# Work on fetched expert rows tied to units of the dense product, and the next norm's rows loaded later

## The chip, the cores and the metric

The kernel runs on one core of a Trainium2 chip. A core has five engines that run side by side: TensorE (PE in the profile; PEld is its weight load), VectorE (DVE), ScalarE (ACT), GpSimd (POOL) and SyncE (SP). Transfers are issued from a queue of SyncE (SPq) or GpSimd (POOLq) and run on 16 shared DMA engines. The metric is the device time of one execution in microseconds; lower is better.

## The reference

Two blocks run one after the other on 256 tokens of width 1024, in float32. The first (two layers of feed-forward, convolution and differential attention) is untouched here. The second has two layers; each is a mixer followed by an expert layer, and the change is in the expert layer:

```
q      = (ht @ w_query).reshape(T, 8, 2, 128)
scores = einsum('thpd,hpkd->thpk', q, sub_keys)          # 128 keys a half
s_top, i_top = top_k(scores, 16)
best, pos    = top_k(s_top[0] + s_top[1], 16)            # all pairs of the two halves
expert_idx   = i_top[0] * 128 + i_top[1]                 # at pos
gates        = softmax(best)
a   = gelu(einsum('tkd,td->tk', expert_u[expert_idx], x)) * gates
out = einsum('tk,tkd->td', a, expert_v[expert_idx])
```

A token so uses 8 x 16 = 128 of 16384 experts; an expert is a row of 1024 numbers in `expert_u` and one in `expert_v`. Between layers stand norms with a gain (and, in the second block, a scale and a shift that depend on a condition vector).

## The kernel before

**Two ways through the experts.** In each expert layer the last 160 tokens (`ND`) go the dense way: all 16384 experts are applied to them. The weights come as 128 units of 128 experts for each of the two products. A unit of the first product is 8 matmuls (16 instructions in the trace, line 1402), a gelu on ScalarE, and later a multiplication with the gates; a unit of the second product is 8 matmuls into three PSUM accumulators (line 1419). The first 96 tokens (`NS`) go the sparse way: `fetch` (line 1321) issues an indirect DMA on GpSimd's queue which brings 128 chosen rows, one to a partition, into one of ten buffers (`NGATHER`), and `fetched` (line 1336) works on a row tile: 96 steps on u (line 1344: multiply with the token's activation and sum) and then 96 steps on v (line 1349: multiply with the gate and add). Step i, once issued, is followed by the fetch for step i + 10, which reuses its buffer.

**What sets the pace.** `sparse(n)` is called after unit n (0 to 127 first product, 128 on second product) and issues steps until their number is 192 (n + 1 - begun - LAG_S) / (250 - begun - LAG_S). A fetch carries a dependence on the last matmul issued before it (`paced[-1]`), so it waits on the chip for that unit. A step carries none: it waits for its row tile alone.

**What sets the order on an engine.** The code issues instructions in program order, but outside the attention stage a scheduler orders each engine's queue by when it estimates an instruction to be ready, earlier program position first. On the chip each queue is worked in that fixed order, and an instruction that waits holds all behind it. `behind` (line 1188) adds an order to such a pair without a wait.

**What runs beside the first product.** VectorE finds the top 16s of the remaining heads and tokens (`halves`, `pick`, `Choice`); these pieces lie in a list with prices (`later`), from which each unit takes 1.3 (`PUMP_U`). The heads of tokens 0 to 127 are chosen in two groups of four. Six units after the last choice the softmax is issued (`LAG_E`, lines 1171 and 1193 to 1195), four units later (`LAG_T`) TensorE transposes indices and gates (lines 1200 to 1202), and then 20 groups of 8 tokens get one-hot tiles on VectorE (lines 1226 to 1229), a gate product on TensorE (1238, 1239), and its application on VectorE and ScalarE (1252, 1254).

**Rows of the next norm.** `gains(ph)` (line 453) loads the gain of the next stage's norm to all partitions (512 KB written) from SyncE's queue and, where the norm has a condition, the scale too; two empty items of 2.0 and then `scaled` (line 466, on VectorE) go to the list; after `scaled` the shift is loaded into the scale's buffer, again from SyncE's queue. Layer 0's expert stage does this for the spatial stage (`sgu`, with scale and shift), layer 1's for the final norm (gain alone). SyncE's queue also issues all weight loads (line 299): 1 MB for two units, into three buffers (`RAW`).

Of the kernel before, what the change touches and what calls it, by code (L numbers as in the profile page):

```python
# [16 lines left out]
ALU = mybir.AluOpType  # L17
# [4 lines left out]
P = 128  # L22
# [25 lines left out]
AFTER = mybir.DependencyInfo(mybir.DependencyClass.Sync, mybir.DependencyReason.SCHED_ONLY)  # L48
# [4 lines left out]
NGATHER = 10  # L53
# [1 line left out]
TOPK = 16  # L55
NCAND = 80
LAG_P, LAG_A = 1, 2
LAG_E, LAG_T, LAG_S = 6, 4, 5
PUMP_Q, PUMP_U = 1.6, 1.3
GSCALE = 2.0 ** 14  # L60
NEG = -3.0e38
# [296 lines left out]
class Kernel:  # L358
# [635 lines left out]
    def peer(s, ph):  # L994
# [9 lines left out]
        V, S, mm = nc.vector, nc.scalar, nc.tensor.matmul  # L1004
        l = int(ph[5:])
        with s.tc.tile_pool(name=ph, bufs=1, reuse_waits="tile") as pp:
            def tl(shape, tag, name=None, dt=F32, bufs=1):
                return pp.tile(list(shape), dt, tag=tag, name=f"{name or tag}_{ph}", bufs=bufs)
# [174 lines left out]
            unit, lagged, gelus = 0, [], []  # L1183
# [98 lines left out]
            ix, z, gate, act = (tl((P, NS), n, dt=d) for n, d in (("ix", U32), ("z", F32), ("eg", F32), ("act", F32)))  # L1282
            steps = [(k, c) for k in 'uv' for c in range(NS)]
            hb, sums, got, paced, known = [], [], [], [], []
            count = 0
# [35 lines left out]
            def fetch(i):  # L1321
                if i < len(steps):
                    kind, c = steps[i]
                    while c // GS not in known:
                        s.pump(1.0)
                    f = nc.gpsimd.indirect_dma_start(out=got[i % NGATHER], out_offset=None, in_=A[f'peer_{kind}'],  # L1326
                                                     in_offset=bass.IndirectOffsetOnAxis(ap=ix[:, c:c + 1], axis=0))
                    if paced:
                        s.tc.add_manual_dep(f.ins, paced[-1].ins.name, AFTER,
                                            reason="a fetch goes with its unit of the dense part")  # L1330

            def acted(c0, c1):
                S.activation(act[:, c0:c1], z[:, c0:c1], AF.Gelu_apprx_tanh)
                V.tensor_tensor(act[:, c0:c1], act[:, c0:c1], gate[:, c0:c1], op=ALU.mult)

            def fetched(n):

                nonlocal count
                while count < min(n, len(steps)):
                    i = count  # L1340
                    (kind, c), row = steps[i], got[i % NGATHER]
                    part = int(c % GS >= 32)
                    if kind == 'u':
                        V.tensor_tensor_reduce(out=row, in0=row, in1=hb[part], scale=1.0, scalar=0.0, op0=ALU.mult,  # L1344
                                               op1=ALU.add, accum_out=z[:, c:c + 1])
                    elif c in (0, 32):
                        V.tensor_scalar(sums[part], row, act[:, c:c + 1], None, op0=ALU.mult)
                    else:
                        V.scalar_tensor_tensor(sums[part], row, act[:, c:c + 1], sums[part], op0=ALU.mult, op1=ALU.add)  # L1349
                    if kind == 'u' and c in (71, 95):  # L1350
                        acted(*((0, GS) if c == 71 else (GS, NS)))
                    fetch(i + NGATHER)
                    count += 1

            first, second = Choice(0, 0, 4, 16), Choice(0, 4, 8, 16)
# [22 lines left out]
            Choice(1, 0, PH, end - 8).queue()  # L1378
            s.later(0.0, chosen.append, 1)
            s.later(0.0, after, LAG_E, softmax)  # L1380
            s.gains(s.following)


            begun, last = [], 2 * P - 6
# [1 line left out]
            def sparse(n):  # L1386

                if known:
                    if not begun:
                        begun.append(n)  # L1390
                        for i in range(NGATHER):
                            fetch(i)
                    fetched(len(steps) * (n + 1 - begun[0] - LAG_S) // (last - begun[0] - LAG_S))
                s.st.ahead()

            for j in range(P):
# [8 lines left out]
                unit = j  # L1405
# [6 lines left out]
            dense = [s.acc(f"acc_{ph}_{i}") for i in range(3)]  # L1412

            def column(c):
                return dense[c // 3][:, (c % 3) * ND:(c % 3 + 1) * ND]

            def add(j, w, ts):
                for c in range(8):
                    paced.append(mm(column(c)[:, ts], w[:, c * P:(c + 1) * P], ring[:, j, ts], start=j == c % 3 == 0,  # L1419
                                    stop=j == P - 1, skip_group_check=True))  # L1420

            for j in range(P - 4):
                add(j, s.st.next(), slice(0, ND))
                sparse(P + j)


            fetched(len(steps))
            s.flush()
            s.next_norm(s.following)
# [6 lines left out]
            out = [s.work(f"out{i}_{ph}") for i in range(2)]  # L1436
# [634 lines left out]
```

## Time and profile before

| | |
|---|---|
| median of 3 runs | 2895.89 us (2894.49 to 2901.7) |
| profiled execution | 2900.55 us, its span 2898.8 us |
| TensorE busy, mean granted clock | 96% of the span, 0.983 |
| VectorE, ScalarE, GpSimd busy | 66%, 33%, 19% |
| first product, layer 0 and layer 1 | starts at 1308.0 and 2239.6 us |
| second product, layer 0 and layer 1 | starts at 1650.7 and ends at 1955 us; layer 1 ends at 2884 us |

The page cuts the span into 40 slices of 72.5 us; the expert layers fill slices 18 to 26 and 31 to 40. A granted clock of 1.00 is 2.4 GHz, 0.50 is 1.2 GHz; a value between is a mean over the stretch. A DMA share near 1 says that the 16 DMA engines were busy all the time. A busy TensorE is not TensorE at its peak, so stretches are compared by how long the same number of matmuls takes.

### The profile page before, as it was taken

How to read it: one execution, taken by the hardware profiler on the slowest of the kernel's cores; microseconds unless marked ns; L12 is line 12 of the kernel's file. 1: busy time of each engine (PE TensorE's matmuls, PEld its weight loads, DVE VectorE, ACT ScalarE, POOL GpSimd, SP SyncE). 2: the span in 40 equal slices, each digit the busy share in tenths (PEclk: the TensorE clock that was granted, in tenths of full speed). 3: DMA queues.
4: the chain of work that ended last, by engine and by line, in shares of the span. 5: the costliest groups of instructions: out<-in, count | busy, mean ns of one | idle time of the engine just before them, and what ended most of it. 6: DMA issues, size and time to landing. Idle time of an engine off the chain costs nothing. (4 is left out here: it accounts for less than half of the span.)

```text
span 2898.8 us, 46472 instructions
## 1 busy us (share of the span) xinstructions
PE 2773.7 (96%) x18628; PEld 2567.5 (89%) x18628; DVE 1903.9 (66%) x3574; ACT 946.2 (33%) x1922; POOL 544.2 (19%) x522
## 2 busy tenths in 40 slices
PE   9999999999999999999789999999999969999998
PEld 7988799899879988889789999997988969999997
DVE  5858785785878676578787544436668878644442
ACT  6457644544654454441121100014444112100000
POOL 0001100000110000004533433310001443334340
PEclk9999999999999999999899999999999989999998
DMA  7844385685438654448989999966444989999994
GB/s 260 329 178 167 139 317 207 224 306 175 168 115 326 214 195 164 170 168 323 370 309 362 415 415 415 413 265 240 175 172 146 382 341 338 368 402 415 415 414 159
DMA packets 146761, 802.44 MB, mean 277 GB/s; under 512 B 18622, under 2 KB 20030, under 8 KB 82281
## 3 DMA queue, kind: packets, MB, share of 16 engines
q1 hardware_dynamic: 87856, 590.67, 54.1%
q0 software_dynamic: 58688, 208.81, 18.7%
q8 instruction: 146, 2.39, 0.3%
q14 instruction: 71, 0.57, 0.1%
HBM read 795.76 MB, written 1.88 MB: 275 GB/s over the span
## 5 line engine op out<-in xcount | busy, mean ns | idle before, releaser
L272 ACT CAST whi<-wraw 128x1024 fp32r<-128x1024 f32 (+1 forms) x508 | 515.2, 1019 | 843.8 <-DMA wraw<-in_w 281.7
L280 DVE TENSOR_TENSOR wlo<-wraw,whi 128x1024 fp32r<-128x1024 f32 (+1 forms) x508 | 597.2, 1181 | 284.1 <-ACT whi L272 282.3
L1402 PE MATMUL pu_peer<-hT_peer,wraw 128*128 128x160 f32 x4096 | 580.6, 303 | 34.0 <-DMA wraw<-in_w 30.0
L1402 PEld LDWEIGHTS pu_peer<-hT_peer,wraw 128*128 128x128 f32 x4096 | 567.5, 193 | 38.6 <-issue 24.9
L1419 PE MATMUL acc_peer<-ring_peer,wraw 128*128 128x160 f32 (+2 forms) x4224 | 583.5, 300 | 13.4 <-DMA wraw<-in_w 11.5
L1419 PEld LDWEIGHTS acc_peer<-ring_peer,wraw 128*128 128x128 f32 x4224 | 576.1, 192 | 21.2 <-DMA wraw<-in_w 15.6
L1349 DVE SCALAR_TENSOR_TENSOR whis_peer<-wlos_peer,act_peer,whis_peer 128x1024 f32<-128x1024 f32 x72 | 92.7, 1287 | 116.5 <-DMA wlos_peer<-in_peer_v,ix_peer 116.4
L628 PE MATMUL pg_ffn<-hhi_first,wlo 128*128 128x256 f32 x576 | 164.4, 285 | 0.0
L627 PE MATMUL pg_ffn<-hlo_first,whi 128*128 128x256 f32 x576 | 163.9, 284 | 0.0
L626 PE MATMUL pg_ffn<-hhi_first,whi 128*128 128x256 f32 x576 | 163.6, 284 | 0.0
L628 PE MATMUL pu_ffn<-hhi_first,wlo 128*128 128x256 f32 x576 | 163.5, 284 | 0.0
L627 PE MATMUL pu_ffn<-hlo_first,whi 128*128 128x256 f32 x576 | 163.2, 283 | 0.0
L626 PE MATMUL pu_ffn<-hhi_first,whi 128*128 128x256 f32 x576 | 162.2, 282 | 0.0
L1344 DVE CUSTOM_DVE_ANT_0 wlos_peer<-wlos_peer,whis_peer 128x1024 f32<-128x1024 f32 x80 | 97.4, 1224 | 61.2 <-DMA wlos_peer<-in_peer_u,ix_peer 60.9
L727 DVE SCALAR_TENSOR_TENSOR ada<-adaw,ca,ada 128x1536 f32<-128x1536 f32 x64 | 116.2, 1816 | 30.4 <-DMA adaw<-in_ada_w 30.3
L1264 ACT ACTIVATE ring_peer<-pu_peer 128x160 f32<-128x160 f32 (+13 forms) x186 | 51.3, 276 | 229.2 <-PE pu_peer L1402 229.2
L1326 POOL DMA_INDIRECT wlos_peer<-in_peer_u,ix_peer x80 | 101.4, 1268 | 110.1 <-PE pu_peer L1402 66.9
L626 PEld LDWEIGHTS pg_ffn<-hhi_first,whi 128*128 128x128 f32 x576 | 109.9, 191 | 4.0 <-issue 1.1
L627 PEld LDWEIGHTS pg_ffn<-hlo_first,whi 128*128 128x128 f32 x576 | 109.5, 190 | 2.8
L628 PEld LDWEIGHTS pg_ffn<-hhi_first,wlo 128*128 128x128 f32 x576 | 109.8, 191 | 0.0
L626 PEld LDWEIGHTS pu_ffn<-hhi_first,whi 128*128 128x128 f32 x576 | 109.2, 190 | 0.0
L628 PEld LDWEIGHTS pu_ffn<-hhi_first,wlo 128*128 128x128 f32 x576 | 108.8, 189 | 0.0
(617 smaller groups left out, 5331.6 us busy)
## 6 DMA issues: line engine op xcount, KB each, us to landing
wraw<-in_w SPq DMA_DIRECT2D x500, 1024.0 KB, 6.7
adaw<-in_ada_w SPq DMA_DIRECT2D x64, 768.0 KB, 7.2
gain_ffn<-in_ffn_norm SPq DMA_DIRECT2D x4, 512.0 KB, 5.6
ring_peer<-in_keysT POOLq DMA_DIRECT2D x2, 1024.0 KB, 5.1
bi_sgu<-in_sgu_b_in POOLq DMA_DIRECT2D x6, 256.0 KB, 7.7
wlos_peer<-in_peer_u,ix_peer POOLq DMA_INDIRECT x80, 10.9
wlos_peer<-in_peer_v,ix_peer POOLq DMA_INDIRECT x72, 12.6
x<-in_x SPq DMA_DIRECT2D x2, 512.0 KB
```

The source lines that it names most:

```text
L272: K.nc.scalar.copy(whi[:, c], s.raw_of(u)[:, c])
L280: K.nc.vector.tensor_tensor(wlo[:, c], s.raw_of(u)[:, c], whi[:, c].bitcast(F32), op=ALU.subtract)
L626: mm(ps, wh, s.hhi[:, k, :], start=k == 0, stop=False)
L627: mm(ps, wh, s.hlo[:, k, :], start=False, stop=False)
L628: mm(ps, wl, s.hhi[:, k, :], start=False, stop=k == 7)
L727: nc.vector.scalar_tensor_tensor(a, raws.pop(i), ca[:, k:k + 1], a, op0=ALU.mult, op1=ALU.add)
L1264: gelus.append(S.activation(slot[:, g:], ps[:, g:], AF.Gelu_apprx_tanh))
L1326: f = nc.gpsimd.indirect_dma_start(out=got[i % NGATHER], out_offset=None, in_=A[f'peer_{kind}'], in_offset=bass.IndirectOffsetOnAxis(ap=ix ...
L1344: V.tensor_tensor_reduce(out=row, in0=row, in1=hb[part], scale=1.0, scalar=0.0, op0=ALU.mult, op1=ALU.add, accum_out=z[:, c:c + 1])
L1349: V.scalar_tensor_tensor(sums[part], row, act[:, c:c + 1], sums[part], op0=ALU.mult, op1=ALU.add)
L1402: paced.append(mm(pu, w[:, k * P:(k + 1) * P], hT[:, k, :], start=k == 0, stop=k == 7))
L1419: paced.append(mm(column(c)[:, ts], w[:, c * P:(c + 1) * P], ring[:, j, ts], start=j == c % 3 == 0, stop=j == P - 1, skip_group_check=True))
```

## The change

- `LAG_S` goes from 5 to 8: the first step comes three units later, and the rate of steps to units rises so that the last step stays where it was.
- Each VectorE step in `fetched` gets the dependence that the fetch has: it waits on the chip for the last matmul issued before it.
- `gains(following)` is no longer called before the first product; it is called at unit 32 (`P // 4`) of the second product, whose loop now takes 1.0 from the list at each unit.

The choice in two groups of heads is the same in both kernels.

```diff
-LAG_E, LAG_T, LAG_S = 6, 4, 5
+LAG_E, LAG_T, LAG_S = 6, 4, 8
...
-                    if paced:
-                        s.tc.add_manual_dep(f.ins, paced[-1].ins.name, AFTER,
-                                            reason="a fetch goes with its unit of the dense part")
+                    pace(f)
+
+            def pace(i):
+
+                if paced:
+                    s.tc.add_manual_dep(i.ins, paced[-1].ins.name, AFTER, reason="paced by the dense part")
...
                     if kind == 'u':
-                        V.tensor_tensor_reduce(out=row, in0=row, in1=hb[part], scale=1.0, scalar=0.0, op0=ALU.mult,
-                                               op1=ALU.add, accum_out=z[:, c:c + 1])
+                        i = V.tensor_tensor_reduce(out=row, in0=row, in1=hb[part], scale=1.0, scalar=0.0, op0=ALU.mult,
+                                                   op1=ALU.add, accum_out=z[:, c:c + 1])
                     elif c in (0, 32):
-                        V.tensor_scalar(sums[part], row, act[:, c:c + 1], None, op0=ALU.mult)
+                        i = V.tensor_scalar(sums[part], row, act[:, c:c + 1], None, op0=ALU.mult)
                     else:
-                        V.scalar_tensor_tensor(sums[part], row, act[:, c:c + 1], sums[part], op0=ALU.mult, op1=ALU.add)
+                        i = V.scalar_tensor_tensor(sums[part], row, act[:, c:c + 1], sums[part], op0=ALU.mult,
+                                                   op1=ALU.add)
+                    pace(i)
...
-                    fetch(i + NGATHER)
+                    fetch(count + NGATHER)
...
             s.later(0.0, after, LAG_E, softmax)
-            s.gains(s.following)
...
             for j in range(P - 4):
                 add(j, s.st.next(), slice(0, ND))
+                if j == P // 4:
+                    s.gains(s.following)
+                s.pump(1.0)
                 sparse(P + j)
```

## Rows read from the trace of the kernel before

**Rows 1.** The page, parts 1 and 2: TensorE's busy time and transfer rate of 40 slices.

```profile
PE 2773.7 (96%) x18628; PEld 2567.5 (89%) x18628; DVE 1903.9 (66%) x3574; ACT 946.2 (33%) x1922; POOL 544.2 (19%) x522
...
GB/s 260 329 178 167 139 317 207 224 306 175 168 115 326 214 195 164 170 168 323 370 309 362 415 415 415 413 265 240 175 172 146 382 341 338 368 402 415 415 414 159
```

**Rows 2.** Windows: stretch, length, busy time of each engine (count), granted clock, DMA share, GB/s.

```profile
1308.00:1326.00 18.00, 13.45 (x99) 13.24 (x98) 18.00 (x117) 3.70 (x8) 8.54 (x13) 0.98 0.69 213
...
1308.00:1467.00 159.00, 130.78 (x929) 129.03 (x928) 125.38 (x486) 23.12 (x67) 77.20 (x77) 0.91 0.91 342
...
2239.00:2394.00 155.00, 128.52 (x929) 125.94 (x929) 125.03 (x487) 22.32 (x67) 75.00 (x77) 0.93 0.89 344
...
1650.00:1903.00 253.00, 246.33 (x1792) 243.36 (x1791) 113.71 (x95) 0.91 (x3) 96.88 (x88) 1.00 1.02 414
2579.00:2831.00 252.00, 246.86 (x1792) 243.45 (x1791) 112.40 (x93) 0.30 (x1) 97.87 (x88) 1.00 1.02 415
2239.00:2354.00 115.00, 108.95 (x791) 107.25 (x791) 95.84 (x432) 18.67 (x53) 58.78 (x56) 1.00 0.95 371
```

**Rows 3.** Windows of line 1402 alone (first product): TensorE, its weight loads, clock, DMA.

```profile
1308.00:1467.00 159.00, 127.09 (x873) 125.00 (x874) 0.91 0.91 342
...
2239.00:2394.00 155.00, 123.53 (x868) 121.20 (x869) 0.93 0.89 344
```

**Rows 4.** Waits of TensorE, 1300 to 1660 us: total us, times, longest.

```profile
PE pu_peer L1402 <- DMA wraw<-in_w: 23.9, 7, 16.2
```

**Rows 5.** Waits of TensorE, 2230 to 2590 us.

```profile
PE pp_peer L1202 <- DVE e_peer L1195: 15.8, 1, 15.8
```

**Rows 6.** Timeline of TensorE, layer 0: start, us, operation, count [idle before, releaser].

```profile
1308.02 13.21 PE L1402 MATMUL pu_peer<-hT_peer,wraw 128*128 128x160 f32 x96
1325.77 16.30 PE L1402 MATMUL pu_peer<-hT_peer,wraw 128*128 128x160 f32 x96 [4.55 <-DMA wraw<-in_w]
...
1388.04 21.97 PE L1402 MATMUL pu_peer<-hT_peer,wraw 128*128 128x160 f32 x160 [1.15 <-DMA wraw<-in_w]
1426.20 17.77 PE L1402 MATMUL pu_peer<-hT_peer,wraw 128*128 128x160 f32 x112 [16.19 <-DMA wraw<-in_w]
```

**Rows 7.** Timeline of TensorE, layer 1, after its long wait.

```profile
2386.37 6.38 PE L1402 MATMUL pu_peer<-hT_peer,wraw 128*128 128x160 f32 x32
...
2393.48 4.57 PE L1402 MATMUL pu_peer<-hT_peer,wraw 128*128 128x160 f32 x32
```

**Rows 8.** Waits of SyncE's DMA queue, 1300 to 1660 us.

```profile
SPq L441 <- DVE gain_sgu L466: 18.6, 1, 18.6
```

**Rows 9.** Timeline of SyncE's queue, layer 0: a row load, three weight loads, the shift.

```profile
1313.30 0.33 SPq L441 DMA_DIRECT2D scale_sgu<-mod  x1
...
1386.92 10.41 SPq L299 DMA_DIRECT2D wraw<-in_w  x3
1415.92 0.33 SPq L441 DMA_DIRECT2D shift_sgu<-mod  x1
```

**Rows 10.** Timeline of VectorE, layer 1, around the softmax's sums (line 1193).

```profile
2344.70 1.23 DVE L1344 CUSTOM_DVE_ANT_0 hhis_peer<-hhis_peer,whis_peer 128x1024 f32<-128x1024 f32 x1 [1.87 <-DMA hhis_peer<-in_peer_u,ix_peer]
...
2367.83 1.23 DVE L1344 CUSTOM_DVE_ANT_0 hlos_peer<-hlos_peer,whis_peer 128x1024 f32<-128x1024 f32 x1
...
2368.98 0.42 DVE L1193 TENSOR_REDUCE sm_peer<-e_peer 128x16 f32<-128x256 f32 x1
```

**Rows 11.** Steps of line 1344, 2239 to 2354 us: duration in ns (min/median/max), starts.

```profile
L1344 DVE CUSTOM_DVE_ANT_0 wlos_peer<-wlos_peer,whis_peer x12: 1197/1220/1226, 2269.3 to 2340.5; 128x1024 f32<-128x1024 f32 x12
```

**Rows 12.** DMA issues of the page: queue, count, KB each, median us to landing.

```profile
wraw<-in_w SPq DMA_DIRECT2D x500, 1024.0 KB, 6.7
...
wlos_peer<-in_peer_v,ix_peer POOLq DMA_INDIRECT x72, 12.6
```

**Rows 13.** Timeline of SyncE's queue in the spatial stage, which loads the same three rows.

```profile
1966.74 0.33 SPq L441 DMA_DIRECT2D scale_peer<-mod  x1
1974.20 0.33 SPq L441 DMA_DIRECT2D shift_peer<-mod  x1
```

More of the change, by code (lines that the diff above doesn't have):

```diff
@@ L1339, in fetched @@
                 while count < min(n, len(steps)):
-                    i = count
-                    (kind, c), row = steps[i], got[i % NGATHER]
+                    (kind, c), row = steps[count], got[count % NGATHER]
                     part = int(c % GS >= 32)
                     if kind == 'u':
-                        V.tensor_tensor_reduce(out=row, in0=row, in1=hb[part], scale=1.0, scalar=0.0, op0=ALU.mult,
-                                               op1=ALU.add, accum_out=z[:, c:c + 1])
+                        i = V.tensor_tensor_reduce(out=row, in0=row, in1=hb[part], scale=1.0, scalar=0.0, op0=ALU.mult,
+                                                   op1=ALU.add, accum_out=z[:, c:c + 1])
                     elif c in (0, 32):
-                        V.tensor_scalar(sums[part], row, act[:, c:c + 1], None, op0=ALU.mult)
+                        i = V.tensor_scalar(sums[part], row, act[:, c:c + 1], None, op0=ALU.mult)
                     else:
-                        V.scalar_tensor_tensor(sums[part], row, act[:, c:c + 1], sums[part], op0=ALU.mult, op1=ALU.add)
+                        i = V.scalar_tensor_tensor(sums[part], row, act[:, c:c + 1], sums[part], op0=ALU.mult,
+                                                   op1=ALU.add)
+                    pace(i)
                     if kind == 'u' and c in (71, 95):
                         acted(*((0, GS) if c == 71 else (GS, NS)))
-                    fetch(i + NGATHER)
+                    fetch(count + NGATHER)
                     count += 1
```

## Prediction

> **What bounds the kernel now.** I read the page first: TensorE is busy 96% of the span, so what counts is where it waits or runs slowly, and the slices with 362 to 415 GB/s are the two expert layers, where transfers may bind as well [rows 1]. Then the windows of those layers. The part of the first product up to about unit 56 has 929 matmuls in both layers and takes 159 and 155 us at a mean clock of 0.91 and 0.93; the second product, until its last fetch, runs at clock 1.00 but with a DMA share of 1.02 and a flat 414 to 415 GB/s [rows 2]. So there are two regimes: holes in the first product, full DMA engines in the second.
>
> The waits of TensorE name the holes. In layer 0 it waits for weights, 16.2 us in one piece [rows 4]; SyncE's queue shows why: the shift row stood 18.6 us at the head of the queue for line 466 [rows 8], so no weight load was issued between the three that end at 1397 and 1416 [rows 9]. Line 466 was late because VectorE had a run of fetched-row steps ahead of it. In layer 1, where the final norm has no shift, that wait is missing, and another stands in its place: 15.8 us of the transposes for the softmax's sums [rows 5]. VectorE's timeline shows the cause: from 2344.70 to 2367.83 it does thirteen steps of line 1344 in a row, waiting for row tiles in the first of them, and line 1193 follows at 2368.98 [rows 10]. By the code's formula they belong to units up to 56, and TensorE stands before unit 52; the scheduler put them there because nothing held them. After either hole the clock is low: 112 matmuls take 17.77 us and 32 take 6.38 us, where 160 take 21.97 and 32 take 4.57 at full clock [rows 6, 7].
>
> **The sum, first product up to unit 56.** Two floors. TensorE's: 873 instructions of line 1402 [rows 3] at 21.97/160 = 0.137 us [rows 6] are 119.9 us, the other matmuls take 130.78 - 127.09 = 3.7 us [rows 2, 3]; together 124 us (layer 1: 868 give 119.2, plus 5.0, again 124). So 35 and 31 us of the 159 and 155 are holes and slow clock. They add up from single rows: in layer 0 the start (4.55 us of wait, then 96 matmuls in 16.30 in place of 13.21: 7.6 us together [rows 6]) and the shift's hole with its slow tail (1.2 + 16.2 of wait and 17.77 - 112 x 0.137 = 2.4 [rows 6], and the rest of the 35, some 7 us: 27); in layer 1 the softmax's hole (15.8) and a slow tail, whose last 32 matmuls alone lose 1.8 [rows 7]; of the other 15 us I put 9 to it: 25.
>
> The transfers' floor: 159 us at 342 GB/s are 54.4 MB [rows 2]. Three row loads of 0.52 MB leave this stretch in layer 0, one in layer 1; and the code's formula (begun at unit 0) gives 38.9 steps at unit 55 with LAG_S 8 where it gave 40.8 with 5, so two fetches of 0.52 MB come later. That leaves 51.8 MB in either layer. The first 18 us, before the rows are known, move only 213 GB/s, 3.8 MB [rows 2]; the other 48.0 MB at 414 GB/s are 116 us: 134 us. Up to ten fetches are in flight at the end, and not all of them must have landed; six of them, 3.1 MB, are 7.6 us: 126 us.
>
> So the transfers come out above TensorE's floor, and late row tiles are how they would be felt: VectorE's idle time of 115 - 95.84 = 19.2 us in 2239 to 2354 [rows 2] ends at row tiles, at 2344.70 by 1.87 us [rows 10]. About thirty steps now stand ahead of line 1193 instead of forty, but the last of these may still come late and hold the transposes for a few us. I take 132 us, near the upper of the two figures, in place of 159 and 155: **-27 and -23 us**. Bounds: -66 together if TensorE's floor were met; -11 if only the start improves (7.6 + 1.3 us, the shift's 27 turning into a softmax hole of 25).
>
> **The cost of the wait.** A step takes 1.22 us [rows 11]. Behind it in VectorE's queue stand the choice, the softmax's sums and the one-hots, for which TensorE's transposes and gate products wait; in the second product only later steps, and the last one (unit 249) is two units, 4.5 us, ahead of the matmul that reads its sum. The next fetch on GpSimd's queue now leaves after the step, some 1.3 us behind its unit; the ten buffers give it 10/0.79 units of 2.26 us, 28 us, against 12.6 us to land [rows 12]. I cost this at nothing; without that cover VectorE would wait, and TensorE only in the first product.
>
> **The sum, second product.** It is bound by transfers [rows 2]: a byte added costs time. A unit is 16 matmuls, 253 us for 1792 [rows 2], 2.26 us. Layer 0 gets three row loads, layer 1 one: 2.1 MB at 414 GB/s, 5 us. One fetch of each layer moves over from the first product (95.2 against 96.4 steps at unit 127) and the rate rises from 0.784 to 0.793 steps a unit: 0.5 MB each, 2.5 us. Then the shift again. The list's credit has grown to its cap of 4.0 by unit 32, so the two empty items go at once and `scaled` follows one unit later, long before the scale has landed; the shift waits on SyncE's queue for landing and `scaled`, with the weight loads behind it. In the spatial stage the same three rows held that queue from 1966.74 to 1974.20, 7.5 us [rows 13]. A weight load has 9 us (two blocks of 4.5) against 6.7 to land [rows 12], 2.3 us of slack, and is due 2.2 us after the hold begins on average: 7.5 to 12 us of hold cost 3 to 7.5. I take 5, nearest to the row of 7.5; bounds 0 and 27, the price of the same hold in the first product. Sum **+13 us**. The two pumped units of list work, and `scaled` itself (1.21 us moved from one VectorE queue place to another with steps alone behind it), cost nothing there. LAG_S itself moves only what is counted above.
>
> The whole: -27 - 23 + 13 = -37 us. The profiled execution took 2900.55 us (2898.8 of span and 1.75 around it), 4.7 above the median; 2900.55 - 37 = 2863.6 there, and **2859 us** for a median like the one shown.
>
> **Rivals.**
> 1. *Transfers bind the first product sooner.* If this mix of rows and weights cannot pass the 371 GB/s of 2239 to 2354 [rows 2], 51.8 MB take 140 us, the gains are 19 and 15, and the time is 2895.9 - 34 + 13 = 2875. For it: row tiles land late there. Against it: the second product has the same mix at 414. The Trainium skill (DMA: Bandwidth & Descriptors, Where 436 GB/s comes from) says that for transfers from HBM the HBM side binds, at about 358 GB/s a core. By that figure the stretch would take 145 us and the time would be about 2885; the trace disagrees, with 414 and 415 GB/s held for 250 us [rows 2].
> 2. *The steps still stand ahead of the softmax's sums,* because the tie does not move them far enough, or late rows hold VectorE as long as now. Layer 0 then trades its shift hole for a softmax hole: -11 + 13, 2898, no change. For it: layer 1 shows that the second hole is there when the first is not [rows 5]. Against it: the run of 2344 to 2368 holds steps of units that TensorE has not reached, which can't be there once tied.
> 3. *The hold of SyncE's queue is as dear in the second product as in the first* (27 us with its clock): 2859 + 22 = 2881. For it: full DMA engines; against it: no steps are ahead of `scaled` that must wait long.
> 4. *Slower: VectorE falls behind by waiting for units.* It is idle 19.2 of 115 us before the softmax [rows 2]. If each of the thirty steps ahead of it waits a whole unit (2.2 us), 66 us, the choice ends 47 us later; the four units of LAG_T take up 9 of that, so 38 us of hole and 9 of slow clock in each layer, 47 against 27 and 25 now: +42 - 9 (starts) + 13, 2942. It decides from about 1.4 us a step (43 us of idle: a hole of 15 and 9 of clock in each layer), where the time equals today's. Against it: a VectorE that is 83% busy there is mostly behind its units, and then finds them done.
>
> **How the numbers follow.** The forecast has 0.61 (own range 2842 to 2874: 126 us in both layers and no hold at the low end, 134 us and a hold of 16 at the high end); rival 1 0.12, rival 2 0.09, rival 3 0.10, rival 4 0.08. A change below 0.3% (8.7 us) can't be told from none here. Forecast, rivals 1 and 3 are faster, 0.83; rival 2 the same, 0.09; rival 4 slower, 0.08. The range of 2842 to 2889 leaves out rivals 2 and 4.
>
> **What would show it.** Right: no `SPq L441` wait between 1300 and 1660; no wait of line 1202 over 3 us in either layer; line 1193 with no run of steps before it; the same 929 matmuls in about 132 us at a clock above 0.97; VectorE's waits in `fetched` now ending at TensorE. In the second product of layer 0 one wait of line 1419 for weights of some 5 us near unit 34, and 257 to 262 us where 253 stood. Wrong: a wait of lines 1202 or 1238 for VectorE above 10 us, or the page's clock row below 9 again in those slices.

## The result, and the profile after

The changed kernel takes 2855.33 us (median of 3 runs, 2850.31 to 2858.32) against 2895.89: ratio 0.9853, 95% interval [0.9822, 0.9883], 40.6 us faster; 2859 was forecast. The profiled execution is the fastest of the three (2850.31, span 2848.6).

The page of the changed kernel, busy times, granted clock and transfer rate of 40 slices, answers to [rows 1]. Each engine has as many instructions as before, and GpSimd is busy 46 us less (498.1 against 544.2). The row of granted clocks, which had an 8 in a slice of each layer's first product (first line below, the kernel before), has no digit under 9 but the last.

```profile
PEclk9999999999999999999899999999999989999998
```

```profile
PE 2767.4 (97%) x18628; PEld 2561.9 (90%) x18628; DVE 1906.8 (67%) x3574; ACT 952.0 (33%) x1922; POOL 498.1 (17%) x522
...
PEclk9999999999999999999999999999999999999998
...
GB/s 271 328 181 170 123 319 213 215 313 185 179 94 307 236 199 165 171 173 256 408 374 376 414 415 414 414 295 240 182 169 169 309 406 372 388 415 416 414 415 164
```

Windows of the changed kernel (columns as in [rows 2]): the first product of layer 0, its start, the first product of layer 1, and the second products.

```profile
1305.00:1445.00 140.00, 128.83 (x938) 126.56 (x937) 113.99 (x473) 23.70 (x70) 58.84 (x71) 0.98 0.94 364
1305.00:1323.00 18.00, 14.45 (x109) 14.21 (x107) 18.00 (x122) 4.38 (x10) 8.75 (x13) 1.00 0.62 193
2212.00:2345.00 133.00, 126.53 (x939) 124.81 (x938) 112.77 (x475) 22.71 (x68) 64.37 (x63) 0.99 0.96 372
1623.00:1876.00 253.00, 245.57 (x1783) 242.25 (x1783) 114.21 (x99) 0.55 (x2) 82.79 (x89) 1.00 1.02 415
2529.00:2781.00 252.00, 246.16 (x1788) 242.84 (x1787) 114.44 (x97) 0.55 (x2) 83.52 (x89) 1.00 1.02 415
```

By the first product's weight loads, the 56 units from the start took 163.2 us in layer 0 and 159.2 in layer 1 before, and take 143.2 and 136.1 now: -20.0 and -23.1. The clock went from 0.91 and 0.93 to 0.98 and 0.99. The second products stand nearly where they stood: windows of 253 and 252 us at 415 GB/s hold 1783 and 1788 matmuls where they held 1792. The first 1792 take 254.5 and 252.9 us from TensorE's first of them, where they took 253.4 and 252.4.

The waits of TensorE, layer 0 (1290 to 1620 us) and layer 1 (2190 to 2545): total, times, longest. The 16.2 us wait of [rows 4] and the 15.8 us wait of line 1202 in [rows 5] are both gone, and nothing over 4.3 us took their place.

```profile
PE pu_peer L1405 <- DMA wraw<-in_w: 10.7, 7, 4.3
...
PE pu_peer L1405 <- DMA wraw<-in_w: 5.5, 7, 2.2
PE pgm_peer L1238 <- DVE obh_peer L1228: 1.4, 1, 1.4
```

VectorE's timeline of layer 0 around the softmax's sums (start, us, operation, [idle before, releaser]) answers to [rows 10]. Line 1193 waits for ScalarE alone, with single steps around it that wait for TensorE, where thirteen steps in a row stood before.

```profile
1421.12 1.23 DVE L1346 CUSTOM_DVE_ANT_0 hlos_peer<-hlos_peer,whis_peer 128x1024 f32<-128x1024 f32 x1 [0.94 <-PE pu_peer L1405]
...
1423.19 0.42 DVE L1193 TENSOR_REDUCE sm_peer<-e_peer 128x16 f32<-128x256 f32 x1 [0.83 <-ACT e_peer L1171]
1423.53 1.22 DVE L1346 CUSTOM_DVE_ANT_0 hlos_peer<-hlos_peer,whis_peer 128x1024 f32<-128x1024 f32 x1
...
1424.95 0.42 DVE L1195 TENSOR_TENSOR e_peer<-e_peer,rs_peer 128x256 f32<-128x256 f32 x1
```

VectorE's waits before the softmax, layer 0 (1300 to 1440 us). The four rows that wait for TensorE are the steps: 23.3 us in fourteen waits, and none for a row tile. (In layer 1, 2210 to 2325, they still wait 13.9 us for row tiles and 2.8 for TensorE.)

```profile
DVE whis_peer L1346 <- PE pu_peer L1405: 8.2, 5, 2.7
DVE wlos_peer L1346 <- PE pu_peer L1405: 5.9, 4, 3.1
DVE hlos_peer L1346 <- PE pu_peer L1405: 4.8, 3, 3.1
DVE hhis_peer L1346 <- PE pu_peer L1405: 4.4, 2, 3.4
```

SyncE's queue in layer 0 shows what was not foreseen. The gain and the scale are issued at 1310.2 and 1311.5 us, at the start of the first product, as before [rows 9]: the loads written into the second product did not move. (The final norm's gain, in layer 1, is likewise issued 4 us into the first product, at 2217.53.)

```profile
1310.19 0.33 SPq L441 DMA_DIRECT2D gain_sgu<-in_norm_mix  x1
1311.52 0.33 SPq L441 DMA_DIRECT2D scale_sgu<-mod  x1
1311.95 43.50 SPq L299 DMA_DIRECT2D wraw<-in_w  x9
1359.13 0.33 SPq L441 DMA_DIRECT2D shift_sgu<-mod  x1
```

The shift still waits there, but shortly (waits of the queue, 1290 to 1620 us):

```profile
SPq L441 <- DVE best_peer L1074: 4.0, 1, 4.0
```

So the start of layer 0 is as slow as in [rows 6]: 96 matmuls, then a wait for weights, then more at a lower clock (82 in 13.06 us at a granted clock of 0.87; 96 take 13.21 at 1.00).

```profile
1306.25 13.21 PE L1405 MATMUL pu_peer<-hT_peer,wraw 128*128 128x160 f32 x96
1323.76 13.06 PE L1405 MATMUL pu_peer<-hT_peer,wraw 128*128 128x160 f32 x82 [4.30 <-DMA wraw<-in_w]
```

### The profile page after: what moved, and what is told of

Its sections match the earlier page's. It is cut to its first block, busy times and chain, and to the rows that moved or that the text cites. A ratio compares the mean times of both kernels' runs of the same rounds, so it can differ in the third digit from the quotient of the medians.

```text
span 2848.6 us, 46660 instructions
## 1 busy us (share of the span) xinstructions
PE 2767.4 (97%) x18628; PEld 2561.9 (90%) x18628; DVE 1906.8 (67%) x3574; ACT 952.0 (33%) x1922; POOL 498.1 (17%) x522
## 5 line engine op out<-in xcount | busy, mean ns | idle before, releaser
L1422 PE MATMUL acc_peer<-ring_peer,wraw 128*128 128x160 f32 (+2 forms) x4224 | 584.0, 301 | 14.7 <-DMA wraw<-in_w 13.9
L627 PE MATMUL pg_ffn<-hlo_first,whi 128*128 128x256 f32 x576 | 163.2, 283 | 0.0
L1262 ACT ACTIVATE h_peer<-pu_peer 128x160 f32<-128x160 f32 (+19 forms) x152 | 40.9, 269 | 234.6 <-PE pu_peer L1405 220.1
L1326 POOL DMA_INDIRECT wlos_peer<-in_peer_u,ix_peer x80 | 94.6, 1182 | 114.8 <-DVE ring_peer L1266 51.9
```

The costliest lines, as they stand in the source:

```text
L627: mm(ps, wh, s.hlo[:, k, :], start=False, stop=False)
```

## The experiments

"First" is the time from TensorE's first weight load of the first product to that of the second product, "second" from there to its last one, layer 0 / layer 1. They come from one profiled execution of each kernel, which lay between 7.3 us below (e9) and 4.7 us above (before) its kernel's median, so small differences in these columns mean little. Ratios are to runs of the kernel before that were timed beside each; its median in those was 2895.89 to 2898.98.

| kernel | median us | ratio, interval | first | second |
|---|---|---|---|---|
| before | 2895.89 | 1 | 342.6 / 340.9 | 304.4 / 303.7 |
| changed | 2855.33 | 0.9853 [0.9822, 0.9883] | 317.6 / 315.8 | 305.5 / 304.2 |
| e1 tie alone | 2854.03 | 0.9851 [0.9830, 0.9872] | 317.4 / 316.4 | 306.1 / 303.0 |
| e2 rows alone | 2902.92 | 1.0015 [1.0003, 1.0027] | 348.9 / 339.2 | 302.2 / 302.3 |
| e3 LAG_S alone | 2895.92 | 0.9994 [0.9983, 1.0004] | 342.2 / 336.9 | 306.4 / 305.8 |
| e4 tie as order only | 2843.74 | 0.9817 [0.9801, 0.9834] | 313.9 / 311.0 | 306.2 / 304.0 |
| e5 rows held to 32 | 2852.30 | 0.9850 [0.9827, 0.9873] | 309.6 / 310.6 | 312.8 / 306.5 |
| e6 rows held to 112 | 2846.40 | 0.9837 [0.9821, 0.9853] | 309.3 / 309.6 | 309.8 / 304.1 |
| e7 held, no tie | 2896.13 | 0.9995 [0.9981, 1.0009] | 338.2 / 338.5 | 309.3 / 301.6 |
| e8 order only, held to 112 | 2845.24 | 0.9826 [0.9809, 0.9842] | 309.9 / 308.2 | 313.1 / 304.8 |
| e9 dot products by order | 2848.90 | 0.9824 [0.9810, 0.9837] | 311.6 / 309.5 | 307.2 / 302.6 |
| e10 accumulations by order | 2845.97 | 0.9818 [0.9804, 0.9831] | 313.6 / 309.6 | 307.6 / 303.8 |
| e11 shift held to 44 | 2849.32 | 0.9830 [0.9814, 0.9847] | 309.0 / 311.0 | 311.0 / 306.3 |
| e12 rows in the gate's units | 2848.50 | 0.9811 [0.9791, 0.9831] | 315.2 / 311.7 | 308.1 / 303.3 |

**The change taken apart (e1, e2, e3).** Each has one part of it, on the kernel before.

```diff
+                    pace(i)                                    # e1 alone
-            s.gains(s.following)                               # e2 alone
+                if j == P // 4: s.gains(s.following)           # e2 alone
+                s.pump(1.0)                                    # e2 alone
-LAG_E, LAG_T, LAG_S = 6, 4, 5
+LAG_E, LAG_T, LAG_S = 6, 4, 8                                  # e3 alone
```

> The kernel before with the tie of the steps alone (LAG_S 5, the next norm's rows asked for before the first product). Theory A (the tie moves the steps behind the softmax's sums and behind the scaled gain, and both holes go): nearly the whole gain, 2850 to 2865 us; no TensorE wait above 6 us in either first product; the shift load held under 5 us in SyncE's queue. Rival B (the gain comes from asking for the rows later): the shift hole of layer 0 stays, only layer 1 gains, about 2870 us. Rival C (the later start of the steps is what helps): no gain, 2890 us or more.

> The kernel before with the rows of the next norm asked for at unit 32 of the second product, no tie, LAG_S 5. Theory A: the scheduler issues the loads where it did, since nothing holds them (they are in the same place of SyncE's queue as before), so no gain: 2887 to 2905 us, and the shift hole of layer 0 stays at 16 us or grows, since `scaled` now stands behind more steps. Rival B: the loads leave the first product, layer 0 gains its shift hole and the start, 2865 to 2880 us.

> The kernel before with LAG_S 8 alone. Theory A: 38 in place of 40 steps stand ahead of the softmax's sums, both holes stay, 2885 to 2900 us. Rival C: three units more for the first rows to land take the waits for row tiles away, and with them a good part of the holes, 2860 to 2880 us.

The tie alone has the whole gain. The other two parts have none (e3 came out as by theory A, e2 is 0.15% slower). SyncE's queue of e2 shows why its loads change nothing, they are issued where they were, and TensorE's waits there (1290 to 1660 us) have the shift's hole again, 21.1 us.

```profile
1313.15 0.33 SPq L441 DMA_DIRECT2D gain_sgu<-in_norm_mix  x1
1314.48 0.33 SPq L441 DMA_DIRECT2D scale_sgu<-mod  x1
```

```profile
PE pu_peer L1404 <- DMA wraw<-in_w: 28.6, 8, 21.1
```

Counted in VectorE's order of instructions, 28 steps stand ahead of the scaling in the kernel before, 35 in e2, 10 in e1 and 7 in the change; ahead of layer 0's softmax's sums 40, 40, 31 and 29.

**The tie without its wait (e4).** The steps are put in the order of their units, 30 of them ahead of the softmax's sums in layer 0, but nothing on the chip waits for the unit. The order is not quite that of the change: 262 of VectorE's 3574 instructions stand at another place.

```diff
-                    pace(i)
+                    pace(i, ORDER)   # as AFTER, without a semaphore
```

> The changed kernel, with the tie of each step to its unit kept for the scheduler's order alone: no wait for TensorE on the chip. Theory A (order is what matters): the steps stand where they stood after the change (30 of them ahead of the softmax's sums), so the time is that of the change within 0.4%, 2845 to 2866 us. Rival D (the wait on the chip is what helps, since it spaces the fetches and keeps transfers from bunching): at least a third of the gain is lost, 2868 us or more.

The order does it: 2843.7, the lowest median here, though its interval overlaps those of all the other tied versions. VectorE's waits of 1300 to 1440 us show that the steps again wait for row tiles, 19.4 us in thirteen waits; TensorE's list of waits for 1300 to 1626 us has none for VectorE.

```profile
DVE wlos_peer L1346 <- DMA wlos_peer<-in_peer_u,ix_peer: 6.4, 4, 2.5
DVE whis_peer L1346 <- DMA whis_peer<-in_peer_u,ix_peer: 5.8, 4, 1.9
DVE hhis_peer L1346 <- DMA hhis_peer<-in_peer_u,ix_peer: 3.9, 2, 2.3
DVE hlos_peer L1346 <- DMA hlos_peer<-in_peer_u,ix_peer: 3.3, 3, 1.9
```

**The rows really moved (e5, e6), without the tie (e7), and with order only (e8).** The gain's and scale's loads get the dependency that the fetches have, so they can't be issued earlier.

```diff
-        s.nc.sync.dma_start(t, ap.partition_broadcast(P))
+        i = s.nc.sync.dma_start(t, ap.partition_broadcast(P))
+        if hold:
+            hold(i)
...
-                    s.gains(s.following)
+                    s.gains(s.following, pace)     # unit 32 (e5); 112 (e6, e7, e8)
```

> The changed kernel with the gain and scale loads of the next norm really held to unit 32 of the second product (each waits for that unit's matmul, as a fetch does); the shift follows on SyncE's queue one weight load later. Theory of the prediction: the first product loses the row loads and starts sooner (-7.6 us in layer 0, -1.3 in layer 1), the second product pays the bytes (5 us) and a hold of SyncE's queue for the shift (5, bounds 0 and 27): 2855 - 9 + 10 = 2856, with one wait of the second product's matmuls for weights of about 5 us near unit 34 of layer 0, and 257 to 262 us in the window of 1792 matmuls that has 253 in the change. Rival (hold as dear as in the first product before): 2855 - 9 + 5 + 27 = 2878. Rival (the rows never cost anything in the first product after the tie; the gain at the start is not theirs): 2855 + 10 = 2865.

> As the run with the hold at unit 32, but at unit 112 of the second product, when only the last fetches are left and transfers bind no more. Theory of the prediction: the start gains -9, the bytes cost nothing there and the hold at most 5: 2846 to 2851. Rival (the start's slow units are not from the rows): 2855, no change. In the trace the wait for weights of 4.3 us after 82 matmuls of layer 0 (at 1323.76) should be gone by the first, and stay by the second.

> The kernel before with the gain and scale loads really held to unit 112 of the second product, and no tie of VectorE's steps: the shift's hold of the first product goes, but forty steps stay ahead of the softmax's sums. Theory (the tie is what the time is won by; without it layer 0 trades its hole for that of layer 1): gain at the start 9 us and little else, 2887, with a wait of line 1202 of 15 to 25 us in both layers. Rival (the hold of SyncE's queue is itself the cost in layer 0): -27 in layer 0, 2896 - 27 = 2869, and a wait of line 1202 in layer 1 alone.

> Both that looked best: the steps ordered by their units without a wait for them on the chip (2843.7 alone, about 10 below the change), and the rows held to unit 112. If the start gains 9 from the rows: 2835 to 2840. If the start is not theirs: 2844 to 2849.

With the rows out, the first product of layer 0 is 8 us shorter than the change's, and 4 shorter with order only (e8 against e4). SyncE's queue of e6 at the start (1306 to 1390 us) is all weights. The 56 units take 134.1 and 134.9 us, 29.1 and 24.3 below before, where the prediction had -27 and -23 with the rows gone. Not all of the 8 us are the rows'. Their effect is clearest in the first 12 units of layer 0 (192 matmuls): those take 33.3 to 36.0 us in the eight kernels that load the gain and the scale there (34.7 before, 33.5 in the change) and 29.2 to 30.5 in the six that load them later, 4.4 us less on average and 3.0 from the change to e6.

```profile
1309.96 75.83 SPq L299 DMA_DIRECT2D wraw<-in_w  x17
```

In the second product the rows cost what was feared in kind: TensorE's timeline of e5 has a wait of 3.70 us for weights, at unit 38, behind the two rows of SyncE's queue. The first 1792 matmuls of layer 0's second product take 259.9 us, where the change has 254.5; 257 to 262 was expected.

```profile
1695.82 8.96 PE L1424 MATMUL acc_peer<-ring_peer,wraw 128*128 128x160 f32 x64 [0.92 <-DMA wraw<-in_w]
1708.48 11.79 PE L1424 MATMUL acc_peer<-ring_peer,wraw 128*128 128x160 f32 x74 [3.70 <-DMA wraw<-in_w]
```

```profile
1693.13 0.44 SPq L441 DMA_DIRECT2D scale_sgu<-mod  x1
1694.92 0.33 SPq L299 DMA_DIRECT2D wraw<-in_w  x1
1706.01 0.33 SPq L441 DMA_DIRECT2D shift_sgu<-mod  x1
1706.43 21.52 SPq L299 DMA_DIRECT2D wraw<-in_w  x6
```

Layer 0's second product is 312.8 us, 7.3 above the change's, and layer 1's 2.3 above; the median is the change's within its interval, so this version trades one for the other. At unit 112 their bytes were expected to cost nothing, but they are not free either: from there to the last matmul e6 takes 55.3 us where the change takes 51.2, with a wait of 2.3 us for weights. Its 2846.4 lies 9 us under the change, in the range expected, but the two intervals overlap.

e7 is the clearest run. The shift's hole is gone from layer 0, and the time is that of before, not the 2887 expected: the first 12 units do gain 5.4 us (34.7 to 29.3), but after unit 112 the rows cost 5.5 (56.8 us against 51.3). TensorE's waits show the softmax's hole in both layers, layer 0 first.

```profile
PE pp_peer L1204 <- DVE e_peer L1197: 13.5, 1, 13.5
...
PE pp_peer L1204 <- DVE e_peer L1197: 16.2, 1, 16.2
```

VectorE's timeline of e7, just before, has steps of later units ahead of the sums, first some that wait for their row tiles, as here, then five in a row until 1436.6.

```profile
1423.90 1.23 DVE L1348 CUSTOM_DVE_ANT_0 wlos_peer<-wlos_peer,whis_peer 128x1024 f32<-128x1024 f32 x1 [2.51 <-DMA wlos_peer<-in_peer_u,ix_peer]
...
1426.42 1.23 DVE L1348 CUSTOM_DVE_ANT_0 wlos_peer<-wlos_peer,whis_peer 128x1024 f32<-128x1024 f32 x1 [1.28 <-DMA wlos_peer<-in_peer_u,ix_peer]
```

e8 (2845.24) is no better than e4, and not at the 2835 to 2840 expected for a gain at the start. The start does gain (the first 12 units 36.0 to 29.2), but the rows take it back in the second product, after unit 112 (51.1 to 57.2). So the rival's range came true for a reason that it did not give.

**Which wait costs ten microseconds (e9, e10).**

```diff
-                    pace(i, ORDER)
+                    pace(i, ORDER if kind == 'u' else AFTER)   # e9
+                    pace(i, AFTER if kind == 'u' else ORDER)   # e10
```

> The changed kernel, with the steps of the first product's rows (the dot products) put in the order of their units without a wait for them on the chip; the accumulating steps keep their wait. The order-only tie of all steps gave 2843.7, the change 2855, and the 10 us between them lay in the first products. Theory (a wait costs where VectorE has other work behind it, in the first product): 2844 to 2846. Rival (it costs wherever fetches wait for steps, the second product too): 2849 to 2855.

> The reverse: the dot products wait for their units on the chip, the accumulating steps are only put in order. By the theory above: 2852 to 2856, like the change. By its rival, or if the ten us are a matter of how one build falls out: 2844 to 2850.

The theory fell: e10, with the dot products' waits, is at 2846, not 2852 to 2856, and e9, without them, at 2848.9, between the theory's 2844 to 2846 and the rival's 2849 to 2855. Moreover e10 and the change have the same instructions in the same order on every engine, and the first 96 steps are dot products, which reach to unit 128. Up to there the two programs do the same, waits included, yet their first products of layer 0 took 317.6 and 313.6 us; the first products of layer 1, whose steps wait alike too, took 315.8 and 309.6. Four to six microseconds of a product are thus execution, not program (in layer 1 the second product ahead of it differs in its waits), and the ten between e4 and the change can't be put down to the wait. What the wait costs stays open, between nothing and 0.4% (0.9853 to 0.9817, intervals that overlap); e1, which has all the waits too, is at 2854, so some cost is likely, but it is not shown.

**The hold of SyncE's queue (e11), and a cheaper place for the rows (e12).** In e11 the scaling is written at unit 44 and not in the list, and the shift's load is held to that unit. e12 does the same at units 68 and 88 of the first product, with the steps tied by order alone. Of e11's edit, on that of e5:

```diff
+        if late:
+            s.scaling = scaled
+            return
...
+                    s.gains(s.following, pace, pace)
+                if j == P // 4 + 12 and s.following in NORMS and NORMS[s.following][2] is not None:
+                    s.scaling()
```

> As the run with the rows held to unit 32 of the second product (2852.3), but the scaling is not left to the list and the shift's load is held to unit 44, some eight weight loads later, when the scaling is long done: the bytes stay, the hold of SyncE's queue goes. If the hold costs what the prediction put on it (5 us): 2847 and a second product of layer 0 of 308 us (it was 312.8 with the hold and 305.5 without the rows), without a wait for weights over 2 us near unit 34. If the bytes alone cost it: 2852 and 312 us.

> Order-only tie, and the rows held to unit 68 of the first product, in the stretch where the gate's products make a unit 2.65 us long and transfers run at 373 to 389 GB/s, with the shift held to unit 88: 34 GB/s below the 414 over 70 us are 2.4 MB, and three rows are 1.6 MB. Theory (what the rows cost is bytes where transfers bind): first products of 309 us as with the later holds, second products of 304 to 306 as without the rows, 2843.7 - 4 - 1 = 2839. Rival (VectorE, busy all of that stretch, has no room for the scaling, or the rows delay weights there): 2844 to 2848.

In e11 SyncE is not held (the shift goes out at 1724.43, after six weight loads), and TensorE's wait is there all the same, 3.69 us:

```profile
1707.24 12.95 PE L1427 MATMUL acc_peer<-ring_peer,wraw 128*128 128x160 f32 x81 [3.69 <-DMA wraw<-in_w]
```

```profile
1692.17 0.43 SPq L441 DMA_DIRECT2D scale_sgu<-mod  x1
1693.96 28.62 SPq L299 DMA_DIRECT2D wraw<-in_w  x6
1724.43 0.33 SPq L441 DMA_DIRECT2D shift_sgu<-mod  x1
```

So that wait comes from the rows ahead of the weights, not from the shift's hold. The hold costs nothing that can be seen: the first 1792 matmuls of layer 0's second product take 259.9 us in both, and the 1.8 us between the whole products (312.8 and 311.0) arise after them. The median, 2849.32, lies between the two that were expected and can't be told from e5's.

e12 missed its 2839: 2848.5, just above the rival's range, with a first product of 315.2, not 309. Its profile shows little of the rival. TensorE waits 2.45 us for the softmax's sums and 3.38 for the one-hots (`obh_peer`), but both come before the rows are issued (1479.89), so the rows are not their cause.

```profile
1423.59 0.33 PE L1207 MATMUL pp_peer<-ident,e_peer 128*128 128x128 f32 x1 [2.45 <-DVE e_peer L1200]
...
1430.90 0.27 PE L1243 MATMUL pgm_peer<-obh_peer,oa_peer 128*128 128x128 f16 x2 [3.38 <-DVE obh_peer L1233]
```

```profile
1479.89 0.33 SPq L441 DMA_DIRECT2D gain_sgu<-in_norm_mix  x1
```

Behind the rows the longest wait is 1.8 us, for weights; from unit 68 to unit 127 e12 takes 143.9 us and e4, without rows there, 140.5. Whether that place is cheaper than the others stays open.

## Why the prediction was right, point by point

- **Which part wins the time: right, and shown.** e1 has all of it. Both holes had one cause, steps ahead of what TensorE needs: with the tie both go, and without it the one becomes the other (e7). Rival 2 had priced that trade at 2898; e7 measured 2896.
- **First products.** Forecast -27 and -23 to unit 56; measured -20.0 and -23.1. Over the whole products it is -25.0 and -25.1 (342.6 to 317.6, 340.9 to 315.8); the rest came in the gate's units after 56, which the sum left out. In layer 0 TensorE waited there for one-hots before (line below, 1300 to 1660 us), and no such wait is left; in layer 1 it fell from 4.3 to 1.4 us. Of the 7 us missing in layer 0 some 3 to 5 are the rows at the start, which were to leave and didn't; the prediction put the start's whole loss of 7.6 [rows 6] to them. The rest is not shown to be the change's: from unit 12 to unit 56 it takes 109.7 us, and e10, the same program up to there, 104.

```profile
PE pgm_peer L1238 <- DVE obh_peer L1228: 5.2, 2, 2.9
```

- **The step that failed: "Three row loads of 0.52 MB leave this stretch".** A load's place in the code is not its place in SyncE's queue: when nothing else holds it, it is issued where it was (in both kernels the gain's load goes out 4.1 us after the first product's first weight load on TensorE). That wipes out the start's gain and the rows' part of the +13 of the second product, bytes and hold, some 10; what was measured is +1.6 in the two layers together (305.5 - 304.4 and 304.2 - 303.7) (the sum had 2.5 for the fetches that move over). Only the shift moved, with the scaling that releases it: 1415.92 [rows 9] to 1359.13, its hold falling from 18.6 us [rows 8] to 4.0.
- **The +13 as a price.** With the rows truly there (e5) the two second products cost 7.3 + 2.3 = 9.6 us more than in the change, close to the 10 put on rows and hold. The parts were not so close: the hold, put at 5, costs nothing visible (e11), and the rows, put at 5, cost 5.4 and 2.1 in the first 1792 matmuls of the two layers (e5 against the change). With the rows out the first products came near the forecast, -29.1 and -24.3 to unit 56 (e6).
- **Rival 1 (transfers bind sooner).** The mean rates of 364 and 372 GB/s look like its 371, but the start lowers them: without its 18 us at 193, layer 0 ran at (140 x 364 - 18 x 193) / 122 = 389, and the second products kept 415. So 371 was no ceiling.
- **The wait at nothing.** VectorE does wait for units, 23.3 us before the softmax in layer 0, and TensorE shows no wait from it: rival 4 would have needed 43. Whether some microseconds remain is open (e4, e10).
- **The signs.** No wait of line 1202 is left, and the clock row and the steps ahead of line 1193 are as forecast. The 929 matmuls take about 132 us in layer 1, as forecast, but 139 in layer 0. VectorE's waits in `fetched` end at TensorE in layer 0, and mostly still at row tiles in layer 1. A wait of 4.0 us for the shift stays on SyncE's queue, and the signs in the second product are absent, as its rows are.
- **Two readings.** The prediction lets all of VectorE's 19.2 us of idle time in layer 1 end at row tiles; in the list of its waits 13.6 do, and 5.6 end at another transfer (`whis_peer<-whis_peer`). And 38.9 and 40.8 steps are what the formula gives at unit 56; at unit 55 it gives 38.1 and 40.0, so the two fetches between them stand.
- **Why the total fits.** In the profiled executions the time fell by 2900.55 - 2850.31 = 50.2 us where 37 was forecast. The first products gave -50.1, but that this is the sum's -27 - 23 is luck: to unit 56, where the sum stops, they gave -43.1. The second products gave +1.6 in place of +13, and 1.8 us of the difference stand already at the start of layer 0's first product, ahead of the change. The profiled execution so lies 13.3 us below its forecast of 2863.6. That the median lies only 3.7 us from 2859 is chance too: the profiled execution of the kernel before was 4.7 us above its median, that of the change 5.0 below.

## What to carry to other kernels

Here steps that nothing tied were put ahead of what mattered, and the engine worked or waited on them. Tie such steps to the work that they are to lie beside, and count what stands ahead of the urgent instruction before and after. A line moved in the code may be no load moved (e2): read the queue's timeline, and hold the load there if it must move (e5). When a hole is closed, ask what was queued behind it: in e7 the next one cost the same.

## What the runs showed that was not expected

The rows of the next norm (0.52 MB each) were free nowhere that the runs show. The two at the start of layer 0's first product cost it some 4.4 us (eight kernels against six), the three at unit 32 of its second product 5.4 (e5 against the change), and the three at unit 112 4.1, 5.5 and 6.1 (e6 against the change, e7 against before, e8 against e4). Two rows at 414 GB/s would take 2.5 us, three 3.8. A single profiled product scattered by 4 to 6 us between programs with the same instructions in the same order, so a difference of 10 us needs more than one execution of each.
